# A decoder layer on one core: a written order for the last token tiles, second-half sums that stay in their PSUM banks, an output projection that opens four banks, and later transposes

## The chip, the cores and the metric

The kernel runs on one core of one Trainium2 chip. The metric is device time in microseconds of one execution, the median of several runs. The engines named here are TensorE (PE, with its weight loads PEld), VectorE (DVE), ScalarE (ACT), GpSimd (POOL) and SyncE (SP, which issues most DMAs).

## The reference

One layer of a hybrid decoder, with 512 tokens, model width 1024, feed-forward width 2816, all in float32:

```
h = h + 0.5 * rmsnorm(swiglu(rmsnorm(h, pre1), W_gu1, W_down1), post1)      # FFN 1
u = rmsnorm(h, mix_pre)
h = h + rmsnorm(token_mixing(u, mem), mix_post)                             # mixing
h = h + 0.5 * rmsnorm(swiglu(rmsnorm(h, pre2), W_gu2, W_down2), post2)      # FFN 2

swiglu(x, W_gu, W_down): g, u = split(x @ W_gu);  (silu(g) * u) @ W_down
token_mixing: y = gate0 * (y_hg @ W_hg) + gate1 * (y_dil @ W_dil) + gate2 * (y_mem @ W_mem);  y @ W_out
```

The three branches of the mixing are a gated linear recurrence, a dilated sliding-window attention and a cross-attention. The last product, `y @ W_out`, is the output projection; it and the ends of both FFNs are what the change touches.

## The kernel before, in words

**Numbers.** Every float32 operand is cut into a high and a low part of type float32r (`split`: ACT copies the high part, DVE subtracts it, line 168 being the DVE helper `tt`, line 173 the ACT copy). A product is three matmuls, high by high, high by low and low by high (`mm3`, line 384). The token axis has NT = 4 tiles of 128 tokens; a model-wide row is two halves (`hf`) of 512 columns; the transposed activations lie in `xhi` and `xlo`.

**FFN.** After a few head columns, `ffn` computes the gate and up products in five stages of four column blocks ("wide" stages, `wide_product`, line 650), with a seven-product scheme whose operands are t1 to t4 and the parts of x. Beside each stage it runs the down product of the stage before (`Down`, line 780): for each half `hf`, four accumulators, one for each token tile, of which three are in the pool `px` (three banks) and the fourth in the pool `ps` (five banks). `evict` adds them to `y` by DVE. The activations of a wide stage are turned by a DVE transpose, a store to DRAM and a read back (`Turn`: lines 817, 825, 830), and `act` cuts them into high and low (line 838).

After the last stage, the down product of its blocks is done tile by tile (`down`, in groups of one tile and one half; FFN 1 adds one block of the stage before, so that a group has 15 matmuls, and 12 in FFN 2). Each group has a bank of `ps`, DVE adds it to `y` (line 168), ACT squares `y` with a running sum (line 186). When both halves of a tile are squared, `rstd` makes the factor: DVE adds (line 192), POOL takes the power (line 195). In FFN 1, DVE multiplies by the gain (line 168), adds the residual (line 266), and `after` spawns the next pre-norm. In FFN 2, `last_tiles` does it: `grow` is a group with its eviction and square, `gained` multiplies by the gain, `final` (line 1016) applies the factor and adds the residual h, `store` writes the tile out.

**Output projection.** `out_proj` cuts the first 512 columns of W_out into the pool `wpool` and the other 512 into the tiles t1 to t4. It forms eight groups (tile, half), each the sum over KD = 8 blocks of features, in the order (0,0) (1,0) (0,1) (1,1) (2,0) (2,1) (3,0) (3,1). Each has a bank of `ps`; ACT squares it, DVE multiplies by the gain; after a tile's second half come the factor, the postnorm and the spawn of the pre-norm for FFN 2. The last branch of the mixing makes the eight features z[0] to z[7] one after another; features 6 and 7 are made last.

**What sets the order.** Parts of the program are tasks (`spawn`) that give the program time at which they go on, in us of planned PE work (`tick`); the table `LAT` holds these delays. `LAT['norm']` is the delay between the spawn of a tile's pre-norm and its transposes (`prenorm`, line 393 on PE, line 204 on DVE for the scaling ahead of them). A scheduler then orders each engine's instructions, earlier in the program first, and takes a later one where the earlier is not ready by its own model. Where `strict` is set, instructions that are pinned (`pin`: DVE, ACT; `fetch`: SP) keep the order of the program. SP issues in order, so an issue that waits for a buffer holds those behind it. Most tiles are `slots`, 37 buffers of 2 KB a partition.

Of the kernel before, what the change touches and what calls it, by code (L numbers as in the profile page):

```python
# [17 lines left out]
P = 128  # L18
# [25 lines left out]
DOWNS = ((0, 1, 0, 1, 0, 1, 1), (0, 0, 2, 2, 2, 1, 1), (0, 0, 2, 2, 1, 0, 0), (0, 0, 1, 1, 1, 0, 0), (0, 0, 1, 0, 1, 0, 0))  # L44

LAT = dict(comb=1.0, mem0=3.5, mem1=8.0, mem2=1.5, mem3=2.0, rest=1.0, hg=1.5, hgx=6.0, hg1=6.0, hg2=11.0, hg3=6.0, hg4=6.0, dil0=4.0, exp=2.0, dil1=9.0, dil2=5.0,
           dil3=3.0, norm=8.0, mnorm=5.0, mload=10.0, start=0.1, step=2.0, keep=2.0)
EARLY, TAIL = 2, 1
HALVES = (slice(0, 512), slice(512, 1024))

# [1 line left out]
class Layer:  # L52
# [415 lines left out]
    def open(self, src, gw, uw, new_act, gu_mm, gu_act, heads, early):  # L468
# [115 lines left out]
            yield 0.1  # L584
            yield from self.combine(t, raw, [pts[t, 0], pts[t, 1]])
        self.spawn(rest(2)), self.spawn(rest(3))

    def copy(self, out, in_, func=AF.Copy):
        ins = self.nc.scalar.activation(out, in_, func)  # L589
        self.pin(ins)  # L590
# [62 lines left out]
    def ffn(self, w_gu, w_down, w_post, ready, reload, after, early, last=False):  # L653
# [24 lines left out]
            return self.slot(dt=F32R), self.slot(dt=F32R)  # L678

        def down(t, hf, cs):  # L680
            acc = self.psum((P, cs.stop - cs.start))
            lhs = act(t)
            for k in [*range(2, n), 0, 1]:
                self.mm3(acc, lhs[k], [x[:, cs] for x in ws[k, hf]], k == 2, k == 1)
            self.tt(y[t][hf][:, cs], y[t][hf][:, cs], acc, ALU.add)

        tail = 0 if last else TAIL
# [111 lines left out]
        def final_load(*fs):  # L799
            for j in fs:  # L800
                rows[j] = self.load(w_down, NF - 4 - tail + j, 1, 0, D)
# [43 lines left out]
        for s in range(len(wides)):  # L845
            end = s == len(wides) - 1
            plan = DOWNS[0 if s == 0 else tail + 2 if end else 1]
            d = Down(f0, n - tail if end else n, act)
            hl = [None] * NT
            turns = [None] * NT  # L850
            self.strict = s > 0
            add = wides[s][1]

            a, u = begun if s == 0 else begin(s)
            cut(s, 2)
            if late:
                late[0]()
            d.load(2)
            if s == 0:
                add(6)  # L860
            for i in range(2):
                self.copy(u[i], a[i])
            if s == 0:
                fetch(s, 7)

            self.wide_product(a, w[s, 2], 2, False)
            cut(s, 6)
            if late:
                late[1]()
            d.make(2)  # L870
            d.load(4)
            add(3)
            fetch(s, 4)
            if late:
                late[2]()
            g = two()
            for i in range(2):
                self.copy(g[i], a[i], AF.Silu)
            d.run(plan[1])

            b = bank()
            self.wide_product(b, w[s, 6], 6)
            cut(s, 5)
            fetch(s + 1, 5)
            d.make(d.done + 3)
            d.load(d.made + 3)
            d.evict()
            for i in range(2):
                self.tt(u[i], u[i], b[i], ALU.add)
            d.run(plan[2])  # L890

            c, p5 = bank(), two()
            self.wide_product(c, w[s, 5], 5)
            cut(s, 7)
            fetch(s + 1, 7)
            d.make(d.done + 2)
            d.load(d.made + 3)
            for i in range(2):
                self.copy(p5[i], c[i])
            cut(s, 4)  # L900
            fetch(s + 1, 1)
            if end:
                final_load(2, 3)
            d.run(plan[3])

            p, v = bank(), two()
            self.wide_product(p, w[s, 7], 7)
            d.make(d.done + 2)
            d.load(d.made + 3)
            d.evict()  # L910
            for i in range(2):
                self.copy(v[i], p[i])
            for i in range(2):
                self.tt(v[i], v[i], p5[i], ALU.subtract)
            cut(s, 3)
            fetch(s + 1, 2)
            if end:
                final_load(*range(4, 4 + tail), 0)
            d.run(plan[4])

            self.wide_product(p, w[s, 4], 4, False)
            d.make(d.done + 2)
            d.evict()
            for i in range(2):
                self.tt(v[i], v[i], u[i], ALU.subtract)
            if end:
                final_cut(2)
                final_load(1)
            cut(s + 1, 1)
            q = two()  # L930
            for i in range(2):
                self.tt(q[i], p[i], u[i], ALU.subtract)
                self.tt(g[i], g[i], q[i], ALU.mult)
                turns[i] = Turn(g[i])
                turns[i].store()
            if end:
                final_cut(*range(3, 4 + tail))
            else:
                wides[s + 1][1](6)
            d.run(plan[5])  # L940

            self.wide_product(c, w[s, 3], 3, False)
            d.make(d.done + (3 if end else 2))
            d.run(plan[6])
            g = two()
            for i in range(2):
                turns[i].back()
            for i in range(2):
                self.tt(g[i], u[i], c[i], ALU.add)
                self.copy(g[i], g[i], AF.Silu)  # L950
                self.tt(g[i], g[i], v[i], ALU.mult)
                turns[2 + i] = Turn(g[i])
                turns[2 + i].store()
            if end:
                for i in range(2):
                    hl[i] = turns[i].act()
                final_cut(0, 1)
                self.opened = turns[3].ins, self.last_act

            def early_rest(turns=turns):  # L960
                for i in range(2, 4):
                    turns[i].back()

            def late_rest(hl=hl, turns=turns):
                for i in range(NT):
                    hl[i] = hl[i] or turns[i].act()
            late = early_rest, d.evict, late_rest
            if end:
                d.run(8)
                late[0](), late[2](), late[1]()  # L970
            else:
                f0, n, act = f0 + n, 4, of_wide(hl)
        self.strict = False
# [1 line left out]
        act = (lambda t: prior(t)[4 - tail:] + fresh(t)) if tail else fresh  # L975
        n = 4 + tail
        h = reload()
        gain = self.bcast_gain(w_post)
        tasks = []
        if last:  # L980
            self.last_tiles(down, y, gain, h, after)
            return tasks
        for t in range(NT):
            whole, parts = slice(0, 512), (slice(0, 256), slice(256, 512))
# [13 lines left out]
            tasks.append(self.spawn(after(h, t)))  # L998
        return tasks

    def last_tiles(self, down, y, gain, h, after):


        whole, parts = slice(0, 512), (slice(0, 256), slice(256, 512))
        z = [[self.slot() for _ in range(2)] for _ in range(NT)]
        ss = [[] for _ in range(NT)]

        def grow(t, hf, cs=whole):
            down(t, hf, cs)
            ss[t].append(self.square(y[t][hf][:, cs], hf, 0.5))  # L1010

        def gained(t, hf, cs=whole):
            self.tt(z[t][hf][:, cs], y[t][hf][:, cs], gain[hf][:, cs], ALU.mult)

        def final(t, r, hf, cs=whole):
            self.pin(self.nc.vector.scalar_tensor_tensor(out=h[t][hf][:, cs], in0=z[t][hf][:, cs], scalar=r, in1=h[t][hf][:, cs], op0=ALU.mult, op1=ALU.add))

        for t in range(NT - 2):
            for hf in range(2):
                grow(t, hf)  # L1020
                gained(t, hf)
            r = self.rstd(ss[t], 0.5)
            for hf in range(2):
                final(t, r, hf)
            after(h, t)
        self.strict = True
        t, u = NT - 2, NT - 1
        grow(t, 0)
        gained(t, 0)
        grow(t, 1)  # L1030
        r = self.rstd(ss[t], 0.5)
        grow(u, 0)
        gained(t, 1)
        grow(u, 1, parts[0])
        final(t, r, 0)
        final(t, r, 1)
        after(h, t)
        grow(u, 1, parts[1])
        self.tt(ss[u][1], ss[u][0], ss[u][1], ALU.add)
        gained(u, 1, parts[0])  # L1040
        r = self.rstd(ss[u][1:], 0.5)
        gained(u, 0)
        gained(u, 1, parts[1])
        final(u, r, 0)
        for cs in parts:
            final(u, r, 1, cs)
        after(h, u)
# [485 lines left out]
    def out_proj(self, z, w_out, w_post, reload, after):  # L1533
# [11 lines left out]
                self.split(hi, lo, st[:, j, :])  # L1545
                w[1].append((hi, lo))
        h = reload()
        for t, hf in [(t, hf) for u in ((0, 1), (2,), (3,)) for hf in range(2) for t in u]:
            ps = self.psum()
            self.proj_N(ps, z, slice(t * P, (t + 1) * P), w[hf])  # L1550
            ss[t][hf] = self.square(ps, hf, 1.0)
            y[t][hf] = self.slot()
            self.tt(y[t][hf], ps, gain[hf], ALU.mult)
            if hf == 1:
                self.postnorm(self.rstd(ss[t], 1.0), y[t], h[t])
                self.post = (t, self.last_v)
                tasks.append(self.spawn(after(h, t)))
# [123 lines left out]
```

## Time and profile before

| what | value |
|---|---|
| median of 3 runs | 1330.68 us (1330.03 to 1332.55) |
| the profiled execution | 1330.72 us, span 1328.9 us |
| PE busy | 1308.1 us (98% of the span) |
| DVE busy | 1056.6 us (80%) |
| ACT busy | 717.5 us (54%) |
| mean granted clock of PE | 0.996 |

All times in the profile are us from the start of the span. A stretch of the table of windows gives the busy time of each engine in it and the granted clock of PE. A row of the timeline gives the start, the length, the engine, the line of the kernel, the instruction with its output and inputs (buffer numbers left out), how many were merged, and in brackets the idle time just before it and the instruction that ended it. FFN 1 ends about 353 us, the mixing and output projection run to 983, FFN 2 to the end.

### The profile page before, as it was taken

How to read it: one execution, taken by the hardware profiler on the slowest of the kernel's cores; microseconds unless marked ns; L12 is line 12 of the kernel's file. 1: busy time of each engine (PE TensorE's matmuls, PEld its weight loads, DVE VectorE, ACT ScalarE, POOL GpSimd, SP SyncE). 2: the span in 40 equal slices, each digit the busy share in tenths (PEclk: the TensorE clock that was granted, in tenths of full speed). 3: DMA queues.
4: the chain of work that ended last, by engine and by line, in shares of the span. 5: the costliest groups of instructions: out<-in, count | busy, mean ns of one | idle time of the engine just before them, and what ended most of it. 6: DMA issues, size and time to landing. Idle time of an engine off the chain costs nothing.

```text
span 1328.9 us, 20915 instructions
## 1 busy us (share of the span) xinstructions
PE 1308.1 (98%) x7545; PEld 1146.1 (86%) x7545; DVE 1056.6 (80%) x1919; ACT 717.5 (54%) x1456; POOL 88.8 (7%) x116
## 2 busy tenths in 40 slices
PE   8999999999999999999999999999999999999997
PEld 8888888887788988899899999999788888888886
DVE  7976979688898975699769968897578768796977
ACT  7644535354577664455765755565366454453442
POOL 1202020100100000000000000000001020202000
PEclk9999999999999999999999999999999999999999
DMA  8679385744725335343223323337634685848434
GB/s 270 184 212 251 127 224 173 207 143 156 243 71 183 117 107 174 111 115 117 65 80 112 113 87 96 104 91 203 208 125 127 184 224 162 242 134 227 151 111 166
DMA packets 190198, 206.00 MB, mean 155 GB/s; under 512 B 12777, under 2 KB 120718, under 8 KB 190094
## 3 DMA queue, kind: packets, MB, share of 16 engines
q1 hardware_dynamic: 175302, 182.57, 43.5%
q0 software_dynamic: 10368, 18.88, 8.0%
q10 hardware_dynamic: 4424, 3.22, 0.8%
q8 instruction: 59, 0.97, 0.3%
q14 instruction: 45, 0.37, 0.1%
HBM read 184.67 MB, written 19.96 MB: 154 GB/s over the span
## 4 chain that ended last, share of the span: by engine, by line
PE 83%; DVE 9%; DMA 2%; ACT 2%; issue 1%; POOL 1%; SPq 0%; POOLq 0%; DVEq 0%; ACTq 0%
PE ps L650 28%; PE ps L384 14%; PE px L780 10%; PE ps L402 7%; PE ps L404 7%; PE ps L403 7%; PE px L389 4%; PE ps L780 3%; DVE s L168 3%; DVE w L168 1%; PE px L393 1%; POOL r L195 1%; ACT s L186 1%; DVE s L204 1%; DVE xlo L168 1%
## 5 line engine op out<-in xcount | busy, mean ns | idle before, releaser
L168 DVE TENSOR_TENSOR w<-st,w 128x512 fp32r<-128x512 f32 x368 | 240.2, 684 | 58.9 <-ACT w L173 56.1
L168 DVE TENSOR_TENSOR s<-s,s 128x512 f32<-128x512 f32 (+3 forms) x347 | 213.1, 633 | 78.7 <-ACT s L589 50.5
L173 ACT ACTIVATE w<-st 128x512 fp32r<-128x512 f32 x360 | 212.5, 626 | 76.4 <-PE ps L403 31.0
L780 PE MATMUL px<-s,s 128*128 128x512 f32 x630 | 154.2, 389 | 0.0
L650 PE MATMUL ps<-w,xhi 128*128 128x512 f32 x480 | 148.9, 391 | 1.5 <-DVE w L168 0.8
L173 ACT ACTIVATE w<-sum 128x512 fp32r<-128x512 f32 x178 | 108.4, 633 | 62.4 <-PE ps L403 46.5
L780 PEld LDWEIGHTS px<-s,s 128*128 128x128 f32 x630 | 118.3, 188 | 24.5
L168 DVE TENSOR_TENSOR w<-sum,w 128x512 fp32r<-128x512 f32 x178 | 119.1, 684 | 19.8 <-ACT w L173 19.4
L589 ACT ACTIVATE s<-ps 128x512 f32<-128x512 f32 x84 | 48.8, 594 | 134.7 <-PE ps L650 134.6
L168 DVE TENSOR_TENSOR s<-s,ps 128x512 f32<-128x512 f32 (+1 forms) x171 | 96.6, 569 | 22.7 <-PE ps L384 17.4
L402 PE MATMUL ps<-xhi,w 128*128 128x256 f32 x384 | 108.8, 283 | 0.0
L404 PE MATMUL ps<-xhi,w 128*128 128x256 f32 x384 | 108.7, 283 | 0.0
L403 PE MATMUL ps<-xlo,w 128*128 128x256 f32 x384 | 108.7, 283 | 0.0
L650 PEld LDWEIGHTS ps<-w,xhi 128*128 128x128 f32 x480 | 89.7, 188 | 21.7 <-DVE w L168 1.8
L650 PE MATMUL ps<-w,xlo 128*128 128x512 f32 x240 | 93.2, 389 | 0.0
L622 POOL DMA_DIRECT2D sum<-in_ffn_w_gu_dram x42 | 38.8, 1069 | 681.5 <-DMA sum<-in_ffn_w_gu_dram 380.0
L384 PE MATMUL ps<-w,xhi 128*128 128x512 f32 x256 | 80.6, 394 | 0.1
L173 ACT ACTIVATE s<-s 128x512 fp32r<-128x512 f32 (+1 forms) x98 | 58.5, 609 | 40.4 <-DMA s<-in_ffn_w_down_dram 30.7
L384 PE MATMUL ps<-s,w 128*128 128x512 f32 (+1 forms) x384 | 80.2, 364 | 0.0
L384 PEld LDWEIGHTS ps<-s,w 128*128 128x128 f32 x384 | 65.0, 189 | 10.7
L402 PEld LDWEIGHTS ps<-xhi,w 128*128 128x128 f32 x384 | 73.6, 192 | 0.7 <-ACT s L411 0.2
L403 PEld LDWEIGHTS ps<-xlo,w 128*128 128x128 f32 x384 | 73.6, 192 | 0.5
(224 smaller groups left out, 3028.9 us busy)
## 6 DMA issues: line engine op xcount, KB each, us to landing
st<-in_ffn_w_gu_dram SPq DMA_DIRECT2D x68, 512.0 KB, 5.0
st<-in_w_in_dram SPq DMA_DIRECT2D x48, 512.0 KB, 3.8
s<-in_ffn_w_down_dram SPq DMA_DIRECT2D x70, 256.0 KB, 5.1
sum<-in_ffn_w_gu_dram SPq DMA_DIRECT2D x50, 256.0 KB, 4.2
sum<-in_ffn_w_gu_dram POOLq DMA_DIRECT2D x42, 256.0 KB, 8.9
turn<-s SPq DMA_DIRECT2D x40, 256.0 KB, 2.1
s<-turn SPq DMA_DIRECT2D x40, 256.0 KB, 2.9
sh<-in_w_in_dram SPq DMA_DIRECT2D x32, 256.0 KB, 3.0
```

The costliest lines, as they stand in the source:

```text
L168: ins = self.nc.vector.tensor_tensor(out=out, in0=a, in1=b, op=op)
L173: self.pin(self.nc.scalar.activation(hi, src, AF.Copy))
L186: self.pin(self.nc.scalar.activation(self.slot(src.shape), src, AF.Square, scale=1.0 / (32.0 * step), accum_out=s))
L384: self.pin_pe(mm(out, lhsT=lhs[l], rhs=rhs[r], start=a, stop=b))
L389: self.nc.tensor.matmul(out, lhsT=lhsT, rhs=rhs, start=start, stop=stop, **k)
L402: mm(out, lhsT=lh, rhs=rh, start=first and k == 0, stop=False, skip_group_check=True)
L403: mm(out, lhsT=lh, rhs=rl, start=False, stop=False, skip_group_check=True)
L404: mm(out, lhsT=ll, rhs=rh, start=False, stop=k == 3, skip_group_check=True)
L589: ins = self.nc.scalar.activation(out, in_, func)
L622: self.nc.gpsimd.dma_start(out=u, in_=x, accum_op=ALU.add)
L650: self.pin(self.nc.tensor.matmul(banks[t], lhsT=l, rhs=r, start=first and k == n == 0, stop=k == 3 and n == 2, skip_group_check=True))
L780: self.pin(nc.tensor.matmul(d.acc[t], lhsT=l[x], rhs=r[z], start=p, stop=q))
```

## The change

In five places:

- The delay `norm` of `LAT` grows from 8 to 13, for the pre-norms behind FFN 1 and behind the output projection.
- `down`: for the second half of tiles 0 to 2, the last groups add onto the banks in which `Down` has left its second-half sums (`accs`), instead of a bank of their own; these three are not evicted in between. The fourth tile's sum is evicted on its own. This holds in both FFNs.
- The gain of the post-norm is loaded ahead, in the last wide stage, behind `final_load` and not after `reload`.
- `last_tiles` (FFN 2) has all four tiles in a written order under `strict`: each tile's finals stand between the two groups of the next tile, and the turned activations of tiles 2 and 3 are cut (`turn`) ahead of group (0,0) and behind group (0,1).
- `out_proj` begins the four groups of tiles 0 and 1 with features 0 to 5, in four banks, then ends them with features 6 and 7 in the order of tiles, and goes on with tiles 2 and 3.

```diff
-           dil3=3.0, norm=8.0, mnorm=5.0, mload=10.0, start=0.1, step=2.0, keep=2.0)
+           dil3=3.0, norm=13.0, mnorm=5.0, mload=10.0, start=0.1, step=2.0, keep=2.0)
...
         def down(t, hf, cs):
-            acc = self.psum((P, cs.stop - cs.start))
+            own = hf == 0 or t == NT - 1
+            acc = self.psum((P, cs.stop - cs.start)) if own else accs[t]
             lhs = act(t)
             for k in [*range(2, n), 0, 1]:
-                self.mm3(acc, lhs[k], [x[:, cs] for x in ws[k, hf]], k == 2, k == 1)
+                l, r = lhs[k], [x[:, cs] for x in ws[k, hf]]
+                for i, j in ((0, 0), (0, 1), (1, 0)):
+                    self.pin_pe(nc.tensor.matmul(acc, lhsT=l[i], rhs=r[j], start=own and k == 2 and i == j == 0, stop=k == 1 and i == 1, skip_group_check=True))
+                self.tick(3 * 0.2158 * (cs.stop - cs.start) / T)
             self.tt(y[t][hf][:, cs], y[t][hf][:, cs], acc, ALU.add)
...
             if end:
                 final_load(*range(4, 4 + tail), 0)
+                gain = self.bcast_gain(w_post)
             d.run(plan[4])
...
             if end:
                 d.run(8)
-                late[0](), late[2](), late[1]()
+                late[0]()
+                accs = d.full.pop()[1]
+                d.evict()
+                self.tt(y[NT - 1][1], y[NT - 1][1], accs[NT - 1], ALU.add)
+                if not last:
+                    late[2]()
...
         h = reload()
-        gain = self.bcast_gain(w_post)
         tasks = []
         if last:
-            self.last_tiles(down, y, gain, h, after)
+            def turn(t):
+                hl[t] = turns[t].act()
+            self.last_tiles(down, y, gain, h, after, turn)
             return tasks
...
+        def factor(t):
+            return self.rstd(ss[t][-2:], 0.5)
+
+        def finals(t, r):
+            final(t, r, 0)
+            final(t, r, 1)
             after(h, t)
+
         self.strict = True
+        r = None
+        for t in range(NT - 1):
+            if t == 0:
+                turn(2)
+            grow(t, 0)
+            if t:
+                finals(t - 1, r)
+            grow(t, 1)
+            if t == 0:
+                turn(3)
+            gained(t, 0)
+            gained(t, 1)
+            r = factor(t)
         grow(u, 0)
-        gained(t, 1)
+        finals(u - 1, r)
         grow(u, 1, parts[0])
-        final(t, r, 0)
-        final(t, r, 1)
-        after(h, t)
+        self.tt(ss[u][1], ss[u][0], ss[u][1], ALU.add)
         grow(u, 1, parts[1])
-        self.tt(ss[u][1], ss[u][0], ss[u][1], ALU.add)
+        gained(u, 0)
+        r = factor(u)
         gained(u, 1, parts[0])
-        r = self.rstd(ss[u][1:], 0.5)
-        gained(u, 0)
         gained(u, 1, parts[1])
         final(u, r, 0)
...
-        for t, hf in [(t, hf) for u in ((0, 1), (2,), (3,)) for hf in range(2) for t in u]:
-            ps = self.psum()
-            self.proj_N(ps, z, slice(t * P, (t + 1) * P), w[hf])
+        acc = {}
+
+        def grow(t, hf, ks):
+            if (t, hf) not in acc:
+                acc[t, hf] = self.psum()
+            ts = slice(t * P, (t + 1) * P)
+            for k in ks:
+                self.mm3(acc[t, hf], (z[k][0][:, ts], z[k][1][:, ts]), w[hf][k], k == 0, k == KD - 1)
+
+        early = [(t, hf) for hf in range(2) for t in range(2)]
+        for t, hf in early:
+            grow(t, hf, range(KD - 2))
+        for t, hf in [(t, hf) for t in range(NT) for hf in range(2)]:
+            grow(t, hf, range(KD - 2, KD) if (t, hf) in acc else range(KD))
+            ps = acc[t, hf]
             ss[t][hf] = self.square(ps, hf, 1.0)
```

The loop of the old `last_tiles` over tiles 0 and 1, outside `strict`, and its lines for tile 2 are removed with it.

More of the change, by code (lines that the diff above doesn't have):

```diff
@@ L999, in ffn, with last_tiles @@
         return tasks
-    def last_tiles(self, down, y, gain, h, after):
+    def last_tiles(self, down, y, gain, h, after, turn):
         whole, parts = slice(0, 512), (slice(0, 256), slice(256, 512))
@@ L1006, in last_tiles @@
         ss = [[] for _ in range(NT)]
+        u = NT - 1
         def grow(t, hf, cs=whole):
```

12 lines of the change are left out of this document (removed).

## Prediction

> **What bounds the kernel now.** I read the page first: is any engine the bound?
>
> ```profile
> span 1328.9 us, 20915 instructions
> PE 1308.1 (98%) x7545; PEld 1146.1 (86%) x7545; DVE 1056.6 (80%) x1919; ACT 717.5 (54%) x1456; POOL 88.8 (7%) x116
> ```
>
> TensorE is busy for 98% of the span, and the change removes no matmul. So all it can win lies in the 20.8 us in which PE is idle and in stretches where PE is busy but slow. Next, the table of busy time by stretch (columns: stretch, length, busy time of PE, PEld, DVE, ACT, POOL, granted clock, DMA share, GB/s), with borders at the stages that the change touches:
>
> ```profile
> 325.00:362.00 37.00, 36.07 (x181) 29.28 (x180) 30.99 (x62) 19.27 (x44) 4.51 (x7) 1.00 0.79 257
> 362.00:395.00 33.00, 31.70 (x196) 27.57 (x195) 31.81 (x59) 23.13 (x49) 2.31 (x4) 1.00 0.27 81
> ...
> 927.16:947.86 20.70, 18.95 (x74) 14.21 (x73) 12.54 (x21) 9.87 (x18) 0.00 (x0) 0.92 0.75 232
> ...
> 983.19:1014.51 31.32, 30.23 (x226) 28.48 (x225) 28.32 (x51) 19.98 (x40) 1.10 (x2) 1.00 0.21 64
> 1297.50:1319.50 22.00, 22.00 (x109) 18.59 (x107) 16.29 (x29) 5.50 (x14) 1.84 (x3) 1.00 0.54 190
> 1319.50:1328.90 9.40, 0.09 (x1) 0.00 (x0) 5.71 (x14) 1.74 (x6) 0.98 (x2) 0.65 0.31 112
> ```
>
> PE idles 0.9 and 1.3 us around the end of FFN 1, 1.75 us at the start of the output projection (there at a mean clock of 0.92), 1.1 us at the start of FFN 2, and 9.3 us after its last matmul. Those are the change's places. The view of waits names the causes, for 325 to 400 us (three rows) and 920 to 1016 us (three more):
>
> ```profile
> PE px L393 <- DVE s L204: 1.1, 3, 0.5
> PE ps L404 <- DVE w L168: 0.5, 1, 0.5
> PE ps L384 <- DVE xlo L168: 0.4, 1, 0.4
> ...
> PE ps L384 <- ACT s L173: 1.7, 2, 0.9
> PE ps L650 <- DVE w L168: 0.6, 1, 0.6
> PE ps L650 <- ACT w L173: 0.4, 1, 0.4
> ```
>
> L393 are the transposes of the pre-norm, L384 at 930 us the output projection, waiting for features 6 and 7 of its input.
>
> **Part 1, output projection.** 192 matmuls stay 192; the evictions, squares and postnorms stay; their order changes. PE in order of time:
>
> ```profile
> 927.16 5.63 PE L384 MATMUL ps<-s,w 128*128 128x512 f32 x24
> 932.63 4.24 PE L384 MATMUL ps<-w,s 128*128 128x512 f32 x18
> 937.76 1.23 PE L384 MATMUL ps<-w,s 128*128 128x512 f32 x3 [0.89 <-ACT s L173]
> 939.82 8.20 PE L384 MATMUL ps<-w,s 128*128 128x512 f32 x27 [0.83 <-ACT s L173]
> 947.86 0.39 PE L384 MATMUL ps<-t2hi,s 128*128 128x512 f32 x1
> ...
> 962.15 1.03 PE L393 MATMUL px<-ident,s 128*128 128x128 f32 x8
> 967.80 1.03 PE L393 MATMUL px<-ident,s 128*128 128x128 f32 x8
> ...
> 980.27 1.03 PE L393 MATMUL px<-ident,s 128*128 128x128 f32 x8
> 983.19 0.28 PE L384 MATMUL ps<-xhi,w 128*128 128x256 f32 x1
> ...
> 992.19 1.04 PE L393 MATMUL px<-ident,s 128*128 128x128 f32 x8
> 996.95 0.28 PE L384 MATMUL ps<-xhi,w 128*128 128x256 f32 x1
> ```
>
> A free-running 512-column matmul costs 2.72/12 = 0.2267 us (first two rows of the last fence below). From 927.16 to 947.86 stand 24+18+3+27 = 72 of them: 16.3 us of work in 20.7, a loss of 4.4 us. 1.72 us are the two waits; most of the rest is the clock, which fell after them:
>
> ```profile
> 941.00:942.00 1.00, 1.00 (x3) 0.81 (x4) 1.00 (x2) 0.28 (x1) 0.00 (x0) 0.50 0.82 211
> ```
>
> In the new order PE has 4 x 18 = 72 matmuls = 16.3 us (932.6 to 949.0) before it needs feature 6. Feature 7's wait ended at 939.82, nine us earlier, so both waits and the dip go. Four banks are open at once, of five: the branch's last ones are read by DVE before the third opens at 940.8. What is late next? Evictions of four groups bunch between 950 and 955, but the banks they free are needed 5 us later. Output projection then ends at 932.63 + 192 x 0.2267 + two sets of transposes (0.79 each, the third moves behind the stage) = 977.7 to 978.0 instead of 983.19.
>
> The Trainium skill, page "TensorE: Matmul & The Clock Gate", part 1, says that the clock halves after an idle window of about 3.4 us. The rows show 0.50 after two idles below 0.9 us, so here the trace does not agree and decides the sum.
>
> **Later transposes at the start of FFN 2.** norm=13 puts a tile's transposes 13 program us (13.7 real, as 0.2158 is planned for 0.2267) behind its spawn, where it was 8. Tiles 0 and 1 finish at 951.7 and 954.4 and transpose about 965 and 969; tile 2 about 980.6, tile 3 about 991: nearly the absolute times of before (962, 968, 980, 992), while the matmuls around them are 5 us earlier. Tiles 0 and 1 are needed at 978 and have 8 us. Tile 3 is needed when the first token half of the heads is over: 978.0 + 96 x 0.12 + 0.79 = 990.3, plus the 1.4 us of the first wide product whose weights are there = 991.7. Its high parts come about 1.5 us after its transposes, so PE will wait about 1 us there; before, that second half began at 996.95. From 983.19 to 1014.51 stand 192 x 0.12 + 24 x 0.2267 + 0.79 = 29.3 us of work: 2.0 us lost. I keep this loss, since the new wait replaces the old ones for weights (1.0 us in the rows above), and add the third transposes: 978.0 + 30.1 + 2.0 = 1010.1, that is **4.4 us** earlier than 1014.51. Ends: 6.4 (no loss) and 1.5 (the wait is 2 us and brings a dip of 1.7 us more, less what overlaps). From 1014 to 1319 PE is never idle, so the lead is kept if weights and DMA shift with it.
>
> **Part 2, end of FFN 1.** The second-half sums of tiles 0 to 2 grow on in their three px banks: the matmuls are as many, three DVE evictions go, the post-norm gain is loaded earlier.
>
> ```profile
> 329.38 1.87 DVE L168 TENSOR_TENSOR s<-s,px 128x512 f32<-128x512 f32 x3
> ...
> 338.34 0.69 DVE L168 TENSOR_TENSOR s<-s,s 128x512 f32<-128x512 f32 x1 [0.84 <-DMA s<-in_ffn_post_w_dram]
> ...
> 370.86 0.63 PE L393 MATMUL px<-ident,s 128*128 128x128 f32 x4 [0.42 <-DVE s L204]
> ```
>
> DVE is spared 1.87 us and the 0.84 us wait. PE's waits here (1.1 + 0.5 + 0.4 = 2.0 us, rows above) are all for DVE, which in 362 to 395 is 96% busy, so PE can win about what DVE wins. The later transposes do not bite: tile 3's ran at 370.86, 17 us after the tail, held by DVE (L204), not by their due time. Ends: 2.0 and -1.0 (transposes that come later than needed by 1 us); I take **1.2**, nearer to the spared 1.87 than to zero. The px banks are given back later, but L393 first needs them at 344, and the second half of tile 0 is evicted about 329.
>
> SP: the two gain issues (about 1 us in all) move ahead of the last weight row, the turn stores and reads, and the eight loads of h. The reads of the first two tiles (SP, landing from the page's DMA issues) and their use by ACT:
>
> ```profile
> 314.26 2.07 SPq L830 DMA_DIRECT2D s<-turn  x2
> ...
> s<-turn SPq DMA_DIRECT2D x40, 256.0 KB, 2.9
> ...
> 321.04 1.13 ACT L838 ACTIVATE s<-s 128x512 fp32r<-128x512 f32 x2
> ```
>
> They land near 318 and have some 3 us to spare, so 1 us costs nothing; what it costs if the gain must wait for slots is a rival below.
>
> **Part 3, end of FFN 2.** The same three evictions go and the order is written out. PE, then DVE, in order of time:
>
> ```profile
> 1297.51 0.39 PE L384 MATMUL ps<-t2hi,s 128*128 128x512 f32 x1
> 1300.23 0.39 PE L384 MATMUL ps<-t2hi,s 128*128 128x512 f32 x1
> ...
> 1308.60 0.69 DVE L168 TENSOR_TENSOR s<-s,ps 128x512 f32<-128x512 f32 x1 [2.04 <-PE ps L384]
> ...
> 1315.87 0.68 DVE L168 TENSOR_TENSOR s<-s,ps 128x512 f32<-128x512 f32 x1
> ...
> 1321.70 0.41 DVE L168 TENSOR_TENSOR s<-s,ps 128x256 f32<-128x256 f32 x1
> ...
> 1322.69 0.21 DVE L192 TENSOR_SCALAR v<-ss,ss 128x1 f32<-128x1 f32 x1 [0.17 <-ACT s L186]
> ...
> 1323.94 1.54 DVE L1016 SCALAR_TENSOR_TENSOR s<-s,r,s 128x512 f32<-128x512 f32 x3
> ```
>
> Seven groups of 2.72 and two of 1.44 put PE's last border at 1319.43. DVE evicts 0.21 us after a border when free (1308.39 to 1308.60), but the last eviction starts at 1321.70: DVE is 2.06 us behind. The first tiles' gain and final steps were bunched after 1308 (idle 2.04 us just before), and tile 2's first eviction, ready at 1311.3, ran at 1315.87. I ran the new order by hand with 0.60 us per DVE step, 0.67 per final step, 0.72 from an eviction to its square, 1.25 from factor to final (1322.69 to 1323.94). The last eight DVE steps: finals of tile 2 at 1317.35, eviction of the first quarter 1318.7, sum of squares 1319.7 (waits for ACT 0.4), last eviction 1319.77, gain 1320.1, factor 1320.76, finals 1322.0. New waits: lo of tile 3 stands behind the square of (0,1) on ACT, and with it the gains of tile 0 on DVE (1.3 us idle at 1304, when nothing is due). Finals at 1322.0 instead of 1323.94: **1.9 us**; ends 2.06 (DVE never late) and 0.9 (it is one step and a factor's 0.5 us late). The 3.4 us of stores behind stay.
>
> **Sum.** 4.4 + 1.2 + 1.9 = 7.5 us. The profiled execution took 1330.72 us (span 1328.9), within 0.04 us of the median 1330.68. 1330.7 - 7.5 = **1323.2 us**.
>
> **Rivals.**
> (a) FFN 2's start gives back more: tile 3's late transposes let PE stand 2 us and the clock dips as at 941. Part 1 shrinks to 1.5: 1326.1 us. For it: the due time moved by 5 us with the stage; against: the scheduler issues transposes early when PE has nothing else ready.
> (b) The clock gate needs a longer idle, and the dip at 941 is not in most runs: then 1.7 us of the 4.4 were never in the median: 1324.9 us. Against: it is in this run, whose time is the median's. That is the gate's rule on the page named above.
> (c) All ends good: 6.4 + 2.0 + 2.06: 1320.2 us. For it: DVE is less loaded in each place.
> (d) The lead is lost between 400 and 1300 us because transfers arrive no earlier. Then only part 3 stays: 1328.8 us. Against: no wait of PE for DMA in either view of waits; issues are released by buffers, which come free earlier too.
> (e) Slower: the gain's two slots. SP issues in order, so if they are not free, the turn stores behind them stand too. For it, this row of the waits, where a slot came free only with a turn store:
>
> ```profile
> POOL s L1359 <- DMA turn<-s: 83.5, 1, 83.5
> ```
>
> If the reads were held by 7 us, from 314 to 321, where that store's slot would come free, PE would stand 4 us beyond the slack and lose 1.7 to the clock, in both FFNs: 11.4 - 7.5 = 3.9 us slower, 1334.6 us. It decides from a hold of about 5 us. Against: I count 32 to 34 live slots of 37 there (y 8, old activations 8, weights 6, and the pairs of the wide product), the gain included.
>
> **How the numbers follow.** Forecast 0.56 (its own range 1321.3 to 1325), (a) 0.15, (b) 0.08, (c) 0.09, (d) 0.06, (e) 0.06. The range from 1320.3 to 1327.3 leaves out (d), (e) and about half of (c). 0.2% is 2.7 us, about what a measurement of this kernel tells from no change, so faster means below 1328.0: forecast, (a), (b), (c): 0.87, with 0.01 off for the edge of (a): 0.86; within: (d) and that edge: 0.08; slower: 0.06.
>
> **What would show it.** Right: no wait for ACT s L173 near 937, clock 1.00 through 930 to 950, transposes L393 without waits for L204, no s<-s,px evictions in threes, the last eviction 0.2 to 0.4 us after the last matmul. Wrong: PE waits for xhi or xlo near 991 with a clock below 1; SP rows of the post-norm gain with long waits; the first idle of PE between 1010 and 1300 for a transfer.

## The result and the profile after

The changed kernel takes 1322.70 us (median of 6 runs, 1322.48 to 1323.84) where the kernel before takes 1330.76 us on the same chip: a ratio of 0.9939, 95% interval 0.9926 to 0.9952. That is 8.1 us less; 7.5 were forecast, to 1323.2 us. Two of the 65 runs of the kernel before that were taken beside the experiments took 2635.80 and 4622.49 us; they are left out of the ratios and of the averages below. The profiled execution took 1322.48 us, its span is 1320.7 instead of 1328.9. The head of its page:

```profile
span 1320.7 us, 20903 instructions
PE 1305.1 (99%) x7545; PEld 1146.2 (87%) x7545; DVE 1053.1 (80%) x1913; ACT 716.6 (54%) x1456; POOL 88.4 (7%) x116
```

The matmuls are the same 7545. PE's idle time went from 20.8 us to 15.6, and its busy time fell by 3.0 us: matmuls at half clock and behind a wait last longer, and these are gone from the output projection. I measured each stage from one matmul to another in both traces:

| stage | before | after | earlier by |
|---|---|---|---|
| start to the first down group of FFN 1 | 321.70 | 322.01 | -0.31 |
| from there to the output projection's first matmul | 610.93 | 609.70 | 1.23 |
| output projection | 50.56 | 45.36 | 5.20 |
| start of FFN 2, to its second wide product | 31.32 | 31.17 | 0.15 |
| from there to the last stage's down groups | 283.00 | 283.28 | -0.28 |
| from there to DVE's last final steps | 26.43 | 24.22 | 2.21 |

They sum to 8.2 us. The same windows in the table of busy time (columns as before; rows: end of FFN 1, output projection, start of FFN 2, down groups of FFN 2, what follows PE's last full group):

```profile
322.01:352.49 30.48, 29.49 (x148) 24.59 (x149) 25.22 (x45) 14.16 (x35) 3.89 (x6) 1.00 0.82 270
931.71:977.07 45.36, 45.36 (x210) 37.67 (x208) 29.28 (x51) 21.76 (x51) 3.63 (x6) 1.00 0.58 189
977.07:1008.24 31.17, 30.83 (x234) 29.18 (x233) 28.61 (x51) 20.92 (x42) 2.30 (x3) 1.00 0.30 85
1291.52:1313.44 21.92, 21.92 (x109) 18.60 (x107) 16.70 (x29) 6.53 (x17) 1.66 (x3) 1.00 0.52 174
1313.44:1320.70 7.26, 0.15 (x2) 0.00 (x0) 3.49 (x9) 0.72 (x4) 0.60 (x1) 0.76 0.34 122
```

In the output projection PE is busy for all of its 45.36 us, at clock 1.00. PE in order of time shows the two waits of before gone, and the transposes (L393) without a bracket, that is, without a wait:

```profile
931.71 8.32 PE L384 MATMUL ps<-w,s 128*128 128x512 f32 x36
939.87 0.39 PE L384 MATMUL ps<-t2hi,s 128*128 128x512 f32 x1
...
965.03 1.03 PE L393 MATMUL px<-ident,s 128*128 128x128 f32 x8
...
967.29 0.60 PE L393 MATMUL px<-ident,s 128*128 128x128 f32 x4
...
971.16 0.60 PE L393 MATMUL px<-ident,s 128*128 128x128 f32 x4
...
977.07 0.28 PE L384 MATMUL ps<-xhi,w 128*128 128x256 f32 x1
...
990.15 1.03 PE L393 MATMUL px<-ident,s 128*128 128x128 f32 x8
...
992.84 0.39 PE L384 MATMUL ps<-xlo,w 128*128 128x256 f32 x1 [0.25 <-DVE xlo L168]
```

At the end, DVE starts the last eviction 0.32 us after PE's last border (1291.52 + 21.92 = 1313.44) instead of 2.27 us after it (1321.70 against 1319.43):

```profile
1313.76 0.42 DVE L168 TENSOR_TENSOR s<-s,ps 128x256 f32<-128x256 f32 x1
...
1314.75 0.21 DVE L192 TENSOR_SCALAR v<-ss,ss 128x1 f32<-128x1 f32 x1
...
1315.74 1.54 DVE L1028 SCALAR_TENSOR_TENSOR s<-s,r,s 128x512 f32<-128x512 f32 x3
```

### The profile page after: what moved, and what is told of

It is laid out like the page before. It is cut to its first block, busy times and chain, and to the rows that moved or that the text cites. A ratio compares the mean times of both kernels' runs of the same rounds, so it can differ in the third digit from the quotient of the medians.

```text
span 1320.7 us, 20903 instructions
## 1 busy us (share of the span) xinstructions
PE 1305.1 (99%) x7545; PEld 1146.2 (87%) x7545; DVE 1053.1 (80%) x1913; ACT 716.6 (54%) x1456; POOL 88.4 (7%) x116
## 4 chain that ended last, share of the span: by engine, by line
PE 89%; DVE 6%; ACT 2%; issue 1%; DMA 1%; POOL 1%; SPq 0%; DVEq 0%; POOLq 0%; ACTq 0%
PE ps L649 27%; PE ps L384 16%; PE px L783 10%; PE ps L402 8%; PE ps L404 8%; PE ps L403 8%; PE px L389 4%; PE ps L783 3%; DVE s L168 2%; PE ps L686 2%; PE px L393 1%; PE px L686 1%; DVE w L168 1%; POOL r L195 1%; ACT s L186 0%
## 5 line engine op out<-in xcount | busy, mean ns | idle before, releaser
L168 DVE TENSOR_TENSOR s<-s,ps 128x512 f32<-128x512 f32 (+1 forms) x165 | 92.8, 566 | 21.9 <-PE ps L384 13.2
```

The costliest lines, as they stand in the source:

```text
L168: ins = self.nc.vector.tensor_tensor(out=out, in0=a, in1=b, op=op)
```

## The experiments

Each kernel's median stands against that of the kernel before in the same series, on one chip. The stage times are from its profile. Stages repeat from kernel to kernel far better than whole runs do: the output projection took 45.36 us in five profiles, the last stage 24.21 or 24.22 in seven.

### Which edit wins the 5.2 us of the output projection

**e1: the new order alone**, in the kernel before, with the delay at 8.

```diff
-        for t, hf in [(t, hf) for u in ((0, 1), (2,), (3,)) for hf in range(2) for t in u]:
+        early = [(t, hf) for hf in range(2) for t in range(2)]
+        for t, hf in early:
+            grow(t, hf, range(KD - 2))
...
```

> The kernel before with the output projection's edit alone (four banks, six features first); the pre-norm delay stays 8. Theory: the gains are local and add up. The 4.4 us between 927 and 948 go (no wait for ACT near 937, clock 1.00), nothing else changes: 1326.3 us, and the span 4.4 to 5 us under that of before. Rival: the lead needs the later transposes; with the delay of 8 they come where the vector engine is not ready, PE waits for them and 2 us or more are given back: 1328 to 1329 us.

1329.36 us against 1329.99, ratio 0.9994 (0.9985 to 1.0002): no gain that can be told from none. The theory fell. PE, then the clock by windows, then DVE and ACT in order of time:

```profile
965.34 0.63 PE L393 MATMUL px<-ident,s 128*128 128x128 f32 x4 [1.14 <-DVE s L204]
...
967.12 0.66 PE L393 MATMUL px<-ident,s 128*128 128x128 f32 x4 [0.93 <-ACT s L222]
```

```profile
964.00:966.00 2.00, 0.86 (x6) 0.58 (x5) 1.56 (x3) 1.01 (x3) 0.40 (x1) 1.00 0.13 46
966.00:968.00 2.00, 1.07 (x7) 0.84 (x7) 2.00 (x4) 1.41 (x3) 0.00 (x0) 1.00 0.00 0
```

```profile
964.43 1.42 DVE L204 SCALAR_TENSOR_TENSOR s<-s,r,s 128x512 f32<-128x512 f32 x2 [0.73 <-POOL r L195]
965.77 0.68 DVE L168 TENSOR_TENSOR xlo<-px,xhi 128x512 fp32r<-128x512 f32 x1
```

```profile
966.48 0.58 ACT L222 COPY s<-px 128x512 f32<-128x512 f32 x1 [1.48 <-DVE xlo L168]
```

The waits near 937 are gone, but two new ones stand 30 us later. In the new order tiles 0 and 1 finish 2.7 us apart (12 matmuls of 0.2267 us), where before 5.4 us lay between them (24 matmuls), and all of their norm work comes together. Tile 1's transposes are due 8 program us after its spawn, and its scaling on DVE (line 204) starts only at 964.43, since it needs squares by ACT, sums by DVE and a power by POOL behind those of tile 0. PE stands 1.14 us. Then it stands 0.93 us more for a bank of px: ACT's copy (line 222) frees it, waits for DVE's low part, and that stands behind line 204. Counted from start to start, where a matmul of 0.39 us is followed by the next after 0.2267 in a free run, the two waits cost 1.31 and 1.17 us: 2.5 of the 4.4 us won are given back.

**e2: the changed kernel with the delay back at 8.**

```diff
-           dil3=3.0, norm=13.0, ...
+           dil3=3.0, norm=8.0, ...
```

> The changed kernel with the pre-norm delay back at 8. Theory: the later transposes are worth little, since before the change the transposes stood where the vector engine let them: 1322.7 us plus 0 to 1 us. Rival: they are what removed PE's waits in both places (the waits for L204, and the 1.0 us at the start of FFN 2): 1324.5 to 1326 us.

1327.19 us, ratio 0.9979 (0.9970 to 0.9988); the span is 4.6 us longer than that of the changed kernel, more than either theory gave. Of these, 3.5 us lie in the output projection and the start of FFN 2. The output projection takes 48.69 us, with e1's two waits. The later transposes, which the prediction had booked as a cost, are what the gain depends on.

**e5: order and delay together**, in the kernel before, nothing else (e1's edit and `norm=13.0`).

> The kernel before with two edits: the output projection in four banks, and the pre-norm delay 13. Theory after the first runs: the two belong together, since four groups that end within 5.4 us bunch the norms of tiles 0 and 1, and a delay of 8 puts tile 1's transposes ahead of its scaling. Together they are worth 5.2 us from the output projection to the start of FFN 2, and the ends of the FFNs the other 2 to 3: 1324.5 to 1325.2 us. Rival: the edits at the ends of the FFNs have a part in the 5.2: 1326 us or more.

1326.40 us against 1330.35, ratio 0.9969 (0.9957 to 0.9981). The output projection takes 45.36 and the start of FFN 2 31.15, as in the full change. The span, 1325.1 us, is 1.6 above 1328.9 less 5.35: the start was 1.1 us and the way to the output projection 0.5 us longer, in code that these edits change only by FFN 1's delay. So the total lies on the rival's side, but the two stages are those of the theory: the ends of the FFNs have no part in them.

**e6: the delay alone**, in the kernel before.

> The kernel before with the delay 13 alone. Theory: in the old order tiles 0 and 1 end 5.4 us apart and their transposes never waited, so a longer delay has nothing to win in the output projection (50.6 us there, less the 0.8 us of a set of transposes that moves into FFN 2): 1330 us, within 0.5 us of before. Rival: the delay wins its 3.5 us by itself, whatever the order: 1326.5 us.

1330.51 us, ratio 1.0005 (0.9996 to 1.0014): nothing, as the theory said. The old waits and the half clock are there again (PE, then the windows):

```profile
937.37 1.23 PE L384 MATMUL ps<-w,s 128*128 128x512 f32 x3 [0.32 <-ACT s L173]
...
939.36 0.73 PE L384 MATMUL ps<-w,s 128*128 128x512 f32 x2 [0.76 <-ACT s L173]
...
940.51 7.43 PE L384 MATMUL ps<-w,s 128*128 128x512 f32 x25 [0.41 <-DVE s L168]
```

```profile
940.00:942.00 2.00, 1.59 (x5) 1.21 (x5) 1.66 (x3) 0.66 (x2) 0.00 (x0) 0.57 0.69 204
942.00:944.00 2.00, 2.00 (x7) 1.57 (x6) 0.00 (x0) 0.03 (x1) 0.00 (x0) 0.58 0.85 196
```

Output projection and start of FFN 2 together (one set of transposes moves between them with the delay, so only the sum compares):

| | delay 8 | delay 13 |
|---|---|---|
| old order | 81.88 (before) | 80.96 (e6) |
| new order | 80.06 (e1), 80.03 (e2) | 76.51 (e5), 76.53 (after) |

The order alone wins 1.8 us of the stage, the delay alone 0.9, both 5.35. The two profiles with the old order contain a stretch of some 3.5 us at half clock, those with the new order none. By an estimate from that length it costs 1.75 us; against a run of the old order without it, the order alone would win next to nothing (80.13 against 80.06) and both edits 3.6 us.

### How late the transposes should be

**e7: the changed kernel with the delay at 10.5** (`norm=10.5`).

> The changed kernel with a delay of 10.5 for 13. In the run with 8, tile 1's scaling was ready 10.4 us behind the end of its last group, and its transposes had been put there after 9.2; 10.5 planned us are 11.0 real ones. Theory (the delay has only to cover this chain): no wait for L204 at 965, at most 0.5 us for the bank, 1322.7 to 1323.5 us. Rival (the more delay the better): half way between 1327.2 and 1322.7, some 1325 us.

1326.25 us, ratio 0.9972 (0.9960 to 0.9983): the rival's side, and beyond its figure. PE in the output projection, and at the start of FFN 2:

```profile
965.84 0.66 PE L393 MATMUL px<-ident,s 128*128 128x128 f32 x4 [1.05 <-ACT s L222]
...
993.56 0.38 PE L384 MATMUL ps<-xhi,w 128*128 128x256 f32 x1 [0.83 <-ACT xhi L173]
994.40 0.39 PE L384 MATMUL ps<-xlo,w 128*128 128x256 f32 x1 [0.46 <-DVE xlo L168]
...
995.55 0.73 PE L649 MATMUL ps<-w,xhi 128*128 128x512 f32 x2 [0.40 <-ACT w L173]
```

The wait for line 204 is gone, that for the bank stays, and tile 3's operands now come too late for FFN 2's second token half: ACT and DVE cut weights and activations there in another order. The two stages take 79.37 us.

**e12: the delay at 16** (`norm=16.0`).

> The changed kernel with the delay of the transposes at 16 instead of 13 (8 lost 4.6 us of span, 10.5 lost 3.0). Theory: 13 is just past the point where PE stops waiting, so 16 wins nothing in out_proj (45.4 us, or 44.6 where eight transposes move behind its end) and costs at the start of FFN 2, which already waits 0.25 us for DVE's low part at 992.84: its first 31 us grow by 1 to 3 us, time 1323.7 to 1325.7 us. Rival: the room at the start of FFN 2 is larger than that wait suggests, and 16 is the same as 13 within 0.5 us, 1322.3 to 1323.2 us.

1327.09 us against 1330.46, ratio 0.9971 (0.9961 to 0.9982). Worse than the theory's range, and mostly in a place that it left out. The output projection takes 46.38 us (0.80 for a px bank at 976.24) and the start of FFN 2 31.92, 0.75 more, but the stretch from FFN 1's end to the output projection grew by 3.4 us, to 613.11, because the delay holds there too. PE, and the clock by windows:

```profile
353.18 0.50 PE L384 MATMUL ps<-w,xlo 128*128 128x512 f32 x1 [1.28 <-DVE xlo L168]
...
361.69 0.80 PE L384 MATMUL ps<-w,xhi 128*128 128x512 f32 x1 [1.93 <-DVE w L168]
```

```profile
362.00:364.00 2.00, 2.00 (x6) 1.52 (x6) 1.56 (x4) 1.12 (x4) 1.42 (x3) 0.50 0.31 118
```

The spans for 8, 10.5, 13 and 16 are 1325.3, 1323.7, 1320.7 and 1325.3 us. Of these four, 13 is the best; 2.5 planned us less cost 3.0 us of span and 3 more cost 4.6. What lies between was not run.

### Which of the two new waits leads, and how many features to run ahead

**e10: e1 with tile 1's transposes in the five banks of ps** instead of the three of px.

```diff
-        for x in self.normed(src, gain, lat, self.psum if self.strict and t == 1 else self.paux):
+        for x in self.normed(src, gain, lat, self.psum if t == 1 else self.paux):
```

> The kernel before with the new order of out_proj alone (delay 8, which lost 1.14 us before tile 1's first transposes and 0.93 us before its second, with the slow starts 1.31 and 1.17) and tile 1's transposes put into the products' banks. Theory: the second wait was for a bank and goes, the first was for the scaling of tile 1 by DVE (line 204) and stays: out_proj's stretch 48.73 -> 47.5 to 47.7 us, time about 1328.0 to 1328.3 us. Rival one: the bank was the cause of both, the stretch is 46.2 us and the time 1326.9. Rival two: the second half's scaling is as late as its bank, the wait is only renamed, and the stretch stays at 48.7 and the time at 1329.2.

1330.91 us, ratio 1.0008 (0.9997 to 1.0019). PE at FFN 1's end, then in the output projection:

```profile
351.21 1.39 PE L393 MATMUL ps<-ident,s 128*128 128x128 f32 x8 [2.81 <-DVE s L204]
...
967.01 1.32 PE L393 MATMUL ps<-ident,s 128*128 128x128 f32 x8 [1.33 <-DVE s L204]
```

In the output projection the theory held in kind: the wait for the bank is gone, the one for line 204 stays, and the stage takes 48.01 instead of 48.73 us (47.5 to 47.7 expected). So the scaling that comes late is a cause of its own. The total went past the expected 1328 because PE now came to tile 1's transposes sooner at FFN 1's end too and stood 2.81 us for line 204 (0.17 before, at 351.69), and the stretch up to the output projection took 613.21 us. Behind that wait the granted clock fell too: it was 0.58 from 352 to 354 and 0.56 from there to 356.

**e8: seven features ahead instead of six**, in the changed kernel.

```diff
-            grow(t, hf, range(KD - 2))
+            grow(t, hf, range(KD - 1))
...
-            grow(t, hf, range(KD - 2, KD) if (t, hf) in acc else range(KD))
+            grow(t, hf, range(KD - 1, KD) if (t, hf) in acc else range(KD))
```

> The changed kernel with seven features ahead and one behind, for six and two. The first group then reaches feature 6 about 4.1 us after its start, when it is 0.9 us late, and feature 7 has 19 us of other work ahead of it. It measures the clock by itself: one wait of 0.9 us, without the second one that stood 2 us later before the change. Theory: the clock fell because two waits came within 3 us; with one it stays at 1.00 and the loss is 0.9 to 1.3 us, 1323.6 to 1324 us. Rival: one short wait suffices, the clock shows 0.5 for 3 us, and 2.5 to 3 us are lost: 1325.2 to 1325.7 us.

1325.35 us, ratio 0.9965 (0.9952 to 0.9977). PE in order of time, and the windows after its first wait:

```profile
937.19 6.01 PE L384 MATMUL ps<-w,s 128*128 128x512 f32 x24 [0.72 <-ACT s L173]
...
974.12 0.66 PE L393 MATMUL px<-ident,s 128*128 128x128 f32 x4 [1.00 <-ACT s L222]
```

```profile
936.00:938.00 2.00, 1.27 (x6) 0.42 (x4) 0.94 (x3) 1.98 (x4) 0.00 (x0) 1.00 0.94 275
938.00:940.00 2.00, 2.00 (x9) 1.66 (x10) 2.00 (x4) 0.96 (x2) 0.00 (x0) 1.00 0.15 44
```

The total is where a half clock would have put it, but the clock stays at 1.00. The 2.5 us of the stage (47.86 against 45.36) are the wait for the feature, 0.72, a new wait for a px bank, 1.00 (with one feature left instead of two, the four groups end even closer together), and what each costs beyond its idle time; some 0.4 us I could not place. Of the two that were run, six features ahead are better than seven, for both reasons.

### The ends of the two FFNs

**e3: the changed kernel without the growing banks** (every group of `down` gets its own bank, and `Down`'s sums are evicted before it).

```diff
-            own = hf == 0 or t == NT - 1
+            own = True
...
-                accs = d.full.pop()[1]
-                d.evict()
-                self.tt(y[NT - 1][1], y[NT - 1][1], accs[NT - 1], ALU.add)
...
+                late[1]()
```

> The changed kernel with a bank of its own for every last group, and the wide sums evicted in threes and one as before (in FFN 2 ahead of the written order). Theory by the prediction's step for FFN 1: the three evictions spared (1.87 us of the vector engine) are most of the 1.2 us there, so 0.8 to 1.2 us are lost in FFN 1, and nothing at the end of FFN 2, where the vector engine has 2.0 and 1.3 us idle after the first evictions: 1323.5 to 1324 us. Rival: the spared evictions are worth nothing, since what moved PE there was the earlier gain: 1322.7 us, the same to 0.3 us.

1322.09 us, ratio 0.9939 (0.9927 to 0.9952): the changed kernel's own ratio. The end of FFN 2 takes 24.21 us, the stretch up to the output projection 609.70, both as with the growing banks. The rival held: beside the other edits, the six evictions spared are worth nothing.

**e4: the changed kernel with the old `last_tiles`** (bank growth and early gain kept).

> The changed kernel with the old order of the last token tiles in FFN 2 (tiles 0 and 1 left to the scheduler, both turned activations cut before); the banks grow on and the gain is loaded early. Theory: the order written out is what keeps the vector engine level with PE; without it the last eviction starts some 1.5 to 2 us behind PE again: 1324.3 to 1324.8 us. Rival: the early gain and the three spared evictions do it, since before the change the vector engine stood idle 2.0 us at 1306 with the gain not landed: 1322.7 to 1323.2 us.

1323.92 us, ratio 0.9954 (0.9942 to 0.9967), between the theory and the rival. The end takes 25.17 us. PE's last border is at 1314.1 there (first down group at 1292.18, and 21.92), and DVE is late by 1.0 us:

```profile
1315.10 0.41 DVE L168 TENSOR_TENSOR s<-s,ps 128x256 f32<-128x256 f32 x1
...
1316.09 0.21 DVE L192 TENSOR_SCALAR v<-ss,ss 128x1 f32<-128x1 f32 x1 [0.17 <-ACT s L186]
```

**e11: the changed kernel with the gain loaded late**, behind the reload of h.

```diff
-                gain = self.bcast_gain(w_post)
...
         h = reload()
+        gain = self.bcast_gain(w_post)
```

> The changed kernel with the gain's two loads and its spread put back behind the reload of h at the end of each FFN, all else as changed. Theory: the end of FFN 2 loses what the early gain was worth beside the order, 24.22 -> 25.4 to 25.5 us (2.21 less the 0.95 of the order), time 1323.8 to 1324.2 us. Rival: with the new order the gain has a longer way to its first use (both halves of a tile are added first), so its place does not matter: 24.2 us and 1322.7 us.

1325.10 us, ratio 0.9957 (0.9945 to 0.9970). The end takes 26.86 us, more than in the kernel before, and more than the theory's 25.5. DVE in order of time:

```profile
1303.95 1.29 DVE L168 TENSOR_TENSOR s<-s,s 128x512 f32<-128x512 f32 x2 [3.80 <-DMA s<-in_ffn_post_w_dram]
```

DVE stands 3.80 us for the gain. In the written order nothing may go past the first multiplication by the gain, so every eviction behind it is late: the last one starts at 1316.65, 3.0 us after PE's last border.

Time from the first down group of FFN 2 to the last final steps:

| | gain late | gain early |
|---|---|---|
| old order of tiles | 26.43 (before) | 25.17 (e4) |
| written order | 26.86 (e11) | 24.22 (after), 24.21 (e3) |

The early gain is worth 1.26 us with the old order (where the two cells differ by the growing banks too, which e3 found to be worth nothing with the written order) and 2.64 with the written one. The order costs 0.43 us with a late gain and wins 0.95 with an early one.

### A version beyond

**e9: e3 with tile 1's transposes in the banks of ps**, aimed at the one wait for a px bank that the changed kernel still has near FFN 1's end (line 225 as in e10). The pools have five and three banks, as told at the start, not the six and two of the expectation.

> The changed kernel, with the second half's banks fresh again (which the run without bank growth showed to be worth nothing) and the transposes of tile 1 put into the six banks of the products instead of the two of their own. Theory: the 0.91 us wait of PE for a transposing bank at 356.31 in the changed kernel (released by ACT's copy of line 222) goes and nothing takes its place: FFN 1's tail and the mixer together 609.70 -> 608.6 to 608.9, out_proj's stretch stays 45.4 us, time 1321.5 to 1322.0 us. Rival: two more of the products' banks are then held by tile 1's halves while they are split by ACT and DVE, a product waits for its bank instead, and the time stays at 1322.5 us or more.

1323.88 us, ratio 0.9948 (0.9930 to 0.9966): not better than the change. PE at the end of FFN 1 and at the start of FFN 2:

```profile
353.22 0.70 PE L384 MATMUL ps<-w,xhi 128*128 128x512 f32 x2 [1.17 <-DVE pcols L168]
...
992.61 0.62 PE L384 MATMUL ps<-xhi,w 128*128 128x256 f32 x3 [0.95 <-ACT xhi L173]
```

The bank's wait went and others came, for DVE and ACT: that stretch takes 610.11 us (609.70) and the start of FFN 2 32.03 (31.17). No version run here beats the changed kernel by more than the noise.

## Why the prediction was right, and where its steps were not

**The total** was right, 1323.2 against 1322.7 us, but in part by luck: part 2 has its size for another reason than the one given, and part 1 rests on an edit that was booked as a cost. The terms 4.4 + 1.2 + 1.9 measure 5.35 + 1.23 + 2.21, less 0.28 given back between 1008 and 1291 and 0.31 of a later start: 8.2.

**Part 1, the output projection.** The 4.4 us between 927 and 948 went as told, and the stage's length, 45.36 us, lies in the 45.1 to 45.4 that its end implied. Both profiles with the old order have the half clock (0.50 in the kernel before and in e6, for some 3.5 us). The mis-sized term is the loss kept at the start of FFN 2: 31.17 less the 30.1 of work is 1.1 us, not 2.0. PE waits there 0.25 us for tile 3's low part, not 1 us for its high part. So 5.35 instead of 4.4.

**Rival (b)**, a half clock that most runs lack, is not ruled out by two profiles. In 63 runs of the kernel before, taken beside the experiments, the mean granted clock goes from 0.994 to 0.998, and the span goes with it: 1331.1 us on average for 4 runs at 0.995, 1329.6 for 21 at 0.996, 1327.4 for 20 at 0.998. The profiled execution has 0.996 and 1328.9. By an estimate from the 3.5 us seen, one such stretch costs a run 1.75 us and 0.0013 of its mean clock. So some runs of the kernel before probably lack it, and there the change wins about that much less. Only a profiled run shows where its clock fell, and the idle end of a run lowers its mean too, so in how many runs it is missing stays open.

**The step that failed in part 1** is "Evictions of four groups bunch between 950 and 955, but the banks they free are needed 5 us later". That looked only at the banks of the sums. What bunches is the whole norm chain of tiles 0 and 1, and its late end, line 204, is awaited by the transposes. The prediction then booked the delay of 13 as a cost to be kept small, with the loss at FFN 2's start. In e1 and e2 it is a condition: without it 3.5 us of the 5.35 are lost. The number came out because the delay was in the change; a reader who had dropped it, following the text, would have had e2's 1327.2 us. "Nearly the absolute times of before" was the right observation (965 and 967 to 971, 978, 990 after; 962, 968, 980, 992 before); its sense was missed: the norm chain had not become 5 us earlier with the matmuls.

**Part 2, FFN 1.** The size, 1.2 us, was met, its reason was not. The prediction took it from DVE's three spared evictions. e3 gives them back and the stretch keeps 609.70 us. Kernels with FFN 1 as before or with the delay alone took 610.9 to 611.95 us there (before, e1, e5, e6), and e1 runs the code of before up to that point, so one profile's noise is about 1 us. But the seven profiles with the early gain and a delay of 8 to 13 (the changed kernel, e2, e3, e4, e7, e8, e9) took 609.70 to 610.11, all less than those four, so the term itself is real. DVE's wait for the gain (0.84 us before, 0.59 in e11) is gone in them. e3, which has there the early gain and the delay but not the growing banks, keeps the whole term, and the delay alone (e5, e6) has none of it, which points to the gain; e11, with the banks and a late gain, took 610.35 in one profile. How the term divides stays open. "The later transposes do not bite" is half right: the waits for line 204 at 344 and 352 went (not by the delay alone, with which e6 still waits 0.83 and 0.29 us), but a wait for a px bank came, the first row of the waits of the changed kernel between 320 and 400 us, and at 16 the delay bites by 3.4 us (e12).

```profile
PE px L393 <- ACT s L222: 0.9, 1, 0.9
```

**Part 3, FFN 2.** 2.21 us instead of 1.9. The last eviction is 0.32 us behind PE as the good end had it, and from factor to final it takes 0.99 us (1314.75 to 1315.74) instead of the assumed 1.25. But the lag was ascribed to the bunched steps of the first tiles alone. e4 and e11 show that the larger part of the win needs the gain to be there early, which the prediction put in part 2 only.

**The rivals.** (a) did not come: FFN 2's start keeps clock 1.00 and loses less than before. (c) did not either: only part 3 passed its good end (2.21 against 2.06), while part 1 and part 2 stayed under theirs (5.35 and 1.23 against 6.4 and 2.0). (d) did not: of the lead, 0.28 us went between 1008 and 1291, and in eight other versions that stretch took 282.91 us, 0.1 less than in the kernel before. The chances of the forecast, (a), (b) and (c) add up to 0.88, not 0.87; nothing hangs on that. (e) did not come: the row given for it ends at 325.33 us, where POOL got its slot, and not at 321, but no hold came. SP issues the gain's loads without one, and the first store of turned activations starts at 311.71 (before, 311.42):

```profile
304.24 0.90 SPq L145 DMA_DIRECT2D s<-in_ffn_post_w_dram  x2
...
311.71 2.75 SPq L828 DMA_DIRECT2D turn<-s  x2
```

## What to carry to other kernels

When a reordering brings the ends of two tiles closer together, follow each tile's whole chain (squares, sums, power, scaling, the copy that frees its bank) to the instruction that waits for it; a delay that fitted the old spacing has to be set anew, and its best value is found by running values on both sides. Edits of one change are seldom additive: run each alone and with its partner before crediting either. In an engine's written order, an operand that arrives late stops everything behind it, so load such operands first (in e11 the gain held DVE for 3.80 us). And a profile is one execution: a cost in it, like the half clock here, need not be paid by every run.

## What the runs showed of the hardware that I had not expected

The granted clock does not follow the length of an idle alone. In the profiles it fell to 0.50, for some 3.5 us each time, after idles of 0.89 and 0.83 us with three matmuls between (before), after 0.32, 0.76 and 0.41 us (e6), after 1.93 us (e12) and after 2.81 us (e10). It stayed at 1.00 after 1.14 and 0.93 us with some matmuls between (e1 and e2), after 1.40 us (e3), after 0.83, 0.46 and 0.40 us (e7), and after 0.72 us (e8). Runs of one program differ as well: those of the kernel before have a mean clock from 0.994 to 0.998. The Trainium skill, page "TensorE: Matmul & The Clock Gate", part 1, has a window of about 3.4 us that runs free of the kernel, and an idle window before the clock halves. None of these idles is 3.4 us long, so the trace does not agree with a window idle throughout; a free-running window could make the same idle cost something or nothing, but no run here tells what decides.
